# Dense matmul steps written between making and using the attention splits, two branches merged through DRAM, and the bonus placed one head pair later

## The chip, the cores and the metric

The kernel runs on one core of a Trainium2 chip. The metric is device time in microseconds (us); the median of several runs counts, and one further execution was profiled. Engine names in the profile: PE is TensorE, PEld its weight load, DVE is Vector, ACT is Scalar, POOL is GpSimd, SP the engine whose queue issues all DMAs here.

## What is computed

One layer of a hybrid decoder trunk on 1024 tokens of width 1024: a token mixer, a cross-attention into 256 memory tokens, a gated FFN and a final norm. The change touches the mixer. One projection of the normalised stream feeds three branches (gated convolution, stick-breaking attention, RWKV-7) and three gates:

```python
proj = xn @ w_comb
y_conv = c_b * causal_dwconv(c_c * c_x, conv_w)
y_sb = stick_breaking_attention(to_heads(q), to_heads(k), to_heads(v))
y_rwkv, v_first = rwkv7_time_mix(proj[..., OFF_RWKV:], ...)
gates = sigmoid(proj[..., OFF_GATE:OFF_RWKV].reshape(b, s, 3, D) + gate_b)
branches = einsum("bsnc,ncd->bsnd", ys, branch_proj)
merged = einsum("bsnd,bsnd->bsd", gates, branches)
h = h + merged @ w_mix_out
```

In the attention of a head, row t weights column s < t by sig(z_ts) times the product of 1 - sig(z_tj) for s < j < t. The RWKV branch adds a bonus: sum over a head of r * k * r_k, times v.

## The kernel before

All large products are made in three parts: each fp32 operand is split into a rounded high part (a cast on ACT) and a low part (a subtraction on DVE or POOL), and hi*hi, hi*lo and lo*hi add up in PSUM. `split_tile` (L234, L235) loads and splits a weight tile in two halves, with raised priority; `dense_fm` (L255, L256, L259) writes the matmuls of one tile of 128 columns by 1024 tokens, six of 128x512 for each of `nk` blocks of 128 rows; `proj` does both for a tile of `w_comb` (`nk` = 8). PSUM holds two tiles `pd` of 1024 columns, for dense products, and four `pq` of 512.

The order is a planner's. The framework's planner takes each engine's instructions from a list in the order of the source (moved up by `high_priority`), and issues the first one whose operands and buffers are ready by its own model of times; on the chip each engine then works its list strictly in order, and waits for what is late. The Python order of the calls is therefore the priority of the work.

The mixer runs in these stages:

- RWKV preparation (about 50 to 240 us): for each of four head pairs p, small products (`small`, L366), three projections (`shifted`: k, r, v), Vector and ACT work between them, and at the end of the pair the bonus: `rkh` and `rkl` (L450, L451) are the split of r * k * r_k, two small products with them and a multiply by v (L455) give `bon`, written to DRAM.
- RWKV recurrence (about 240 to 600 us), with 24 filler tiles (`FILL_R`) behind it in the source, 12 gate tiles and 12 of the memory's keys and values, which the planner pulls into its gaps.
- Stick-breaking attention, four head pairs (about 620 to 1207 us). `sb_proj(p)` projects v, k and q of a pair and splits them. `sb_att(p)` goes over 2 heads and 4 row blocks m of 256 rows: `scores` (L814, L815 on PE, sigmoids on ACT, masks on POOL, a scan L825 and a multiply L827 on DVE) makes two tiles Z, and `weighted` (of the block before, by the list `late`) transposes Z (L837), splits it into `ah` (L841, ACT) and `al` (L842, DVE) and multiplies by v (L847, L848). Behind each of the pairs 0 to 2 the source has `sb_proj` of the next pair and `fill(5)`: the other 12 gate tiles and 4 convolution tiles of three projections each. `gate_tile` writes its sigmoid to `gate_d` in DRAM, `conv_tile` its result to `y_d[0]`.
- Before pair 3 the residual tiles `h` (x, 8 of 512 KB) are loaded into the room of `xn`, which is done with. Merge: in the order `MERGE` = conv, RWKV, attention, `branch_y` loads a branch's result from `y_d` and splits it (L746, L747), `branch` makes a product (`nk` = 4) for each of 8 column tiles and loads its gate tile. The first branch's gated tiles stay in SBUF (`acc`, multiply L902), the second's are multiplied (L934) and added on POOL (L935), the third's (`merged`, L943, L944) complete the sum, which is split again (L947, L948) and multiplied by `w_mix_out` in `accumulate`, two tiles at a time, into `h` (L921).

Cross-attention and FFN follow and are left as they are.

## Time and profile before

| | |
|---|---|
| median of 3 runs | 2392.54 us (2390.92 to 2396.98) |
| profiled execution, device time | 2392.83 us |
| its span, first to last instruction | 2390.7 us |
| PE busy (matmuls) | 2232.4 us, 93% |
| DVE busy | 1464.3 us, 61% |
| ACT busy | 894.3 us, 37% |
| POOL busy | 541.3 us, 23% |
| mean granted clock of PE | 0.975 of full speed |
| DMA | 222 MB, 28.6% of the 16 engines' span |

Matmuls overlap in the pipeline, so a row's duration (0.39 us for 128x512) is longer than the distance between two starts; idle time of PE is what no matmul covers. The granted clock is a mean between full (1.0, 2.4 GHz) and half (0.5, 1.2 GHz).

### The profile page before, as it was taken

The page shows a single profiled execution, that of the slowest core. Times are in us where ns is not written, and L with a number is a line of the kernel's source. Part 1 is how long each engine was busy: PE and PEld are TensorE (multiplying, and loading weights), DVE is VectorE, ACT ScalarE, POOL GpSimd, SP SyncE. Part 2 cuts the span into 40 slices and gives each one's busy share as a digit, 9 for nine tenths or more (in the row PEclk, how much of TensorE's full clock was granted, in tenths as well). Part 3 has the DMA queues.
Part 4 walks back from the last instruction along what each step waited for, and adds up shares of the span by engine and source line. Part 5 has one row for each costly group of instructions (what it writes and reads, how often), then busy time and mean ns, then how long its engine had stood idle before and what let it go on. Part 6 is the DMA issues. An engine that isn't in the chain of part 4 may idle for free.

```text
span 2390.7 us, 29984 instructions
## 1 busy us (share of the span) xinstructions
PE 2232.4 (93%) x11635; PEld 1838.1 (77%) x11635; DVE 1464.3 (61%) x2017; ACT 894.3 (37%) x1493; POOL 541.3 (23%) x465
## 2 busy tenths in 40 slices
PE   6998899999989898999799999998699999999998
PEld 5776788878868687788677888886588888877887
DVE  7566555673281816311856675547988888867535
ACT  6643233434362625311622134224444444442212
POOL 1123221222121222122212000001644444413000
PEclk9999999999999999999999999999799999999999
DMA  4323534522302121112465112101322222155211
GB/s 152 128 93 128 192 96 122 155 72 93 93 18 80 36 71 54 55 60 71 154 216 163 56 32 68 32 26 71 89 88 80 87 82 80 62 171 186 96 42 71
DMA packets 225792, 222.15 MB, mean 93 GB/s; under 512 B 34804, under 2 KB 187634, under 8 KB 224626
## 3 DMA queue, kind: packets, MB, share of 16 engines
q1 hardware_dynamic: 225649, 220.24, 28.6%
q8 instruction: 91, 1.49, 0.3%
q14 instruction: 52, 0.42, 0.1%
HBM read 162.00 MB, written 58.20 MB: 92 GB/s over the span
## 4 chain that ended last, share of the span: by engine, by line
PE 69%; DVE 13%; issue 9%; ACT 3%; DMA 3%; POOL 2%; SPq 0%; POOLq 0%; DVEq 0%; ACTq 0%
PE pd L255 8%; PE pd L256 7%; PE pd L259 7%; PE pd L915 5%; PE pd L916 5%; PE pd L919 5%; PE pd L1174 3%; PE pd L1176 3%; PE pd L1175 3%; PE pq L1176 2%; PE pq L1174 2%; PE pq L1175 2%; DVE B L825 2%; DVE wl L235 1%; PE pq L848 1%
## 5 line engine op out<-in xcount | busy, mean ns | idle before, releaser
L255 PE MATMUL pd<-xn_hi,wh 128*128 128x512 f32 x960 | 382.1, 398 | 7.4 <-ACT ft L481 7.4
L256 PE MATMUL pd<-xn_lo,wh 128*128 128x512 f32 x960 | 380.1, 396 | 0.0
L234 ACT CAST wh<-wr 128x512 fp32r<-128x512 f32 x270 | 158.8, 620 | 517.3 <-issue 179.2
L259 PE MATMUL pd<-xn_hi,wl 128*128 128x512 f32 x960 | 306.0, 396 | 0.1
L235 DVE TENSOR_TENSOR wl<-wr,wh 128x512 fp32r<-128x512 f32 x166 | 127.2, 790 | 189.7 <-ACT wh L234 189.5
L235 POOL TENSOR_TENSOR wl<-wr,wh 128x512 fp32r<-128x512 f32 x104 | 139.1, 1354 | 386.3 <-ACT wh L234 383.1
L921 DVE TENSOR_TENSOR h<-pd,h 128x1024 f32<-128x1024 f32 x120 | 146.5, 1220 | 128.8 <-PE pd L919 128.6
L255 PEld LDWEIGHTS pd<-xn_hi,wh 128*128 128x128 f32 x960 | 182.8, 190 | 45.1 <-ACT ft L481 7.8
L256 PEld LDWEIGHTS pd<-xn_lo,wh 128*128 128x128 f32 x960 | 182.8, 190 | 36.3
L259 PEld LDWEIGHTS pd<-xn_hi,wl 128*128 128x128 f32 x960 | 180.7, 190 | 37.5 <-POOL wl L235 0.8
L915 PE MATMUL pd<-wh,ah 128*128 128x512 f32 x352 | 139.6, 397 | 9.5 <-DVE h L921 5.7
L916 PE MATMUL pd<-wl,ah 128*128 128x512 f32 x352 | 139.3, 396 | 1.8 <-DVE wl L1254 1.8
L1168 DVE TENSOR_TENSOR wp<-ws,wp 128x512 fp32r<-128x512 f32 x88 | 120.9, 1374 | 2.4 <-ACT wp L1167 1.8
L1174 PE MATMUL pd<-b,wp 128*128 128x512 f32 x264 | 106.8, 405 | 3.9 <-ACT wp L1167 2.4
L919 PE MATMUL pd<-wh,al 128*128 128x512 f32 x352 | 110.0, 394 | 0.0
L1174 PE MATMUL pq<-t,wp 128*128 128x512 f32 x264 | 103.1, 391 | 2.9 <-ACT wp L1167 2.9
L1111 POOL TENSOR_TENSOR t<-h,t 128x512 fp32r<-128x512 f32 x12 | 17.7, 1482 | 385.1 <-ACT t L1110 385.1
L1227 POOL TENSOR_TENSOR h<-h,h 128x1024 f32<-128x1024 f32 x22 | 52.8, 2400 | 227.7 <-DVE h L1192 193.1
L1176 PE MATMUL pd<-b,wp 128*128 128x512 f32 x264 | 104.0, 394 | 0.2 <-DVE wp L1168 0.2
L1175 PE MATMUL pd<-b,wp 128*128 128x512 f32 x264 | 104.0, 394 | 0.0
L1175 PE MATMUL pq<-t,wp 128*128 128x512 f32 x264 | 102.9, 390 | 0.0
L1167 ACT CAST wp<-ws 128x512 fp32r<-128x512 f32 x88 | 54.7, 622 | 128.5 <-POOL ws L1160 65.8
(366 smaller groups left out, 5154.1 us busy)
## 6 DMA issues: line engine op xcount, KB each, us to landing
wr<-in_w_comb_dram SPq DMA_DIRECT2D x124, 256.0 KB
raw<-in_ffn_up_dram SPq DMA_DIRECT2D x88, 256.0 KB
gate_d<-ft SPq DMA_DIRECT2D x24, 512.0 KB
hid_d<-h SPq DMA_DIRECT2D x22, 512.0 KB
wr<-in_ffn_down_dram SPq DMA_DIRECT2D x42, 256.0 KB
t<-hid_d SPq DMA_DIRECT2D x21, 512.0 KB
wr<-in_ca_wkv_dram SPq DMA_DIRECT2D x32, 256.0 KB
gt<-gate_d SPq DMA_DIRECT2D x16, 512.0 KB
```

Source lines behind the costliest of these rows:

```text
L234: s_.copy(hi[:, sl], raw)
L235: (v_ if lo_e == "dve" else g_).tensor_tensor(lo[:, sl], raw, f32(hi[:, sl]), ALU.subtract)
L255: pe.matmul(o, wh(k), xh(k, h), start=k == 0, stop=False)
L256: pe.matmul(o, wh(k), xl(k, h), start=False, stop=False)
L259: pe.matmul(o, wl(k), xh(k, h), start=False, stop=k == nk - 1)
L915: pe.matmul(ps[:, cs], ah[:, tk], wh[:, cs], start=k == 0, stop=False)
L916: pe.matmul(ps[:, cs], ah[:, tk], wl[:, cs], start=False, stop=False)
L919: pe.matmul(ps[:, cs], al[:, tk], wh[:, cs], start=False, stop=k == n - 1)
L921: v_.tensor_tensor(h[i], ps, h[i], ALU.add)
L1174: pe.matmul(ps, wh[:, k, :], xh[:, k, :], start=k == 0, stop=False)
L1175: pe.matmul(ps, wh[:, k, :], xl[:, k, :], start=False, stop=False)
L1176: pe.matmul(ps, wl[:, k, :], xh[:, k, :], start=False, stop=k == 3)
```

## The change

- **Bonus.** The bonus of RWKV head pair p becomes a function that is called after the k projection of pair p + 1; the last one is called after the loop.
- **Dense steps.** `dense_steps` is `dense_fm` as a generator that yields after each block of six matmuls. `conv_tile`, `sb_proj` and the gate tiles become jobs: a column of `w_comb` and a function that uses the product. `Stream` holds a list of jobs, loads the next job's weights when it begins one, and `beside(work)` runs a generator and, at each of its yields, as many dense steps as its rate says; what is left at the end follows. `sb_att` is a generator that yields after each `scores` (16 times a pair) and inside `weighted` (20 times). `weighted` now makes the transposes and split of turn jj + 1 before the products of turn jj and yields in between.
- **Order.** Behind the recurrence stand only the 24 tiles of `FILL`. Beside pair p stand the jobs of `FILL_S[p]`: p is a projection of the next pair, g a gate tile, c a convolution tile of three projections; 12, 12 and 9 projections. All weight splits of these have their low part on POOL; before, those of `sb_proj` were on DVE.
- **Merge.** Beside pair 3 run the products of the first two branches (conv and RWKV): their inputs `y0` and `y2` lie in the room of `xn`, with six buffers `mt`; each gated product is written to `acc_d` in DRAM (16 of 512 KB). `h` is now loaded after pair 3, in the room of `y2`. `merged` loads both tiles from `acc_d` (16 reads), adds them on POOL and goes on as before; `mg` has 6 buffers instead of 4.

```diff
-FILL = "gm" * 12 + "g" * 12 + "cccc"
-FILL_R = 24
-FILL_S = 5
+FILL = "gm" * 12
+FILL_S = ("pcpgpcgg", "pcpgpcgg", "pgpgpgggg")
        ...
+        acc_d = dram.tile([2, KD, P, T], F32, name="acc_d")
        ...
+        def dense_steps(ps, wh, wl, xh, xl, nk):
+
+            for k in range(nk):
+                for h in range(2):
+                    o = ps[:, h * 512:(h + 1) * 512]
+                    pe.matmul(o, wh(k), xh(k, h), start=k == 0, stop=False)
+                    pe.matmul(o, wh(k), xl(k, h), start=False, stop=False)
+                for h in range(2):
+                    o = ps[:, h * 512:(h + 1) * 512]
+                    pe.matmul(o, wl(k), xh(k, h), start=False, stop=k == nk - 1)
+                yield k
        ...
                 k = shifted(4 + p, 4 + p, "k")
+                if bonus:
+                    bonus.pop()()
        ...
-                bon = kp.tile([P, T], F32, name="gt", bufs=2)
-                small(lambda t, ps: v_.tensor_tensor(bon[:, t], ps, vv[:, t], ALU.mult),
-                      (bmr, rkh), (bmr, rkl))
-                dma(bon_d[:, p, :], bon)
+                def add_bonus(p=p, rkh=rkh, rkl=rkl, vv=vv):
+                    bon = kp.tile([P, T], F32, name="gt", bufs=2)
+                    small(lambda t, ps: v_.tensor_tensor(bon[:, t], ps, vv[:, t], ALU.mult),
+                          (bmr, rkh), (bmr, rkl))
+                    dma(bon_d[:, p, :], bon)
+                bonus.append(add_bonus)
+            bonus.pop()()
        ...
+        def conv_jobs(j):
        ...
+            return [(W + j * P, first), (2 * W + j * P, second), (j * P, third)]
+        def gate_job(n, j):
+            def use(ps):
+                t = ftp.tile([P, T], F32, name="ft")
+                s_.activation(t, ps, AF.Sigmoid, bias=col("gate_b", n * KD + j))
+                dma(gate_d[n, j], t)
+
+            return OFF_GATE + n * D + j * P, use
        ...
+        def proj_run(job):
+            c0, use = job
+            def load():
+                return split_tile(wf, w_comb[:, :, c0:c0 + P], [P, KD, P], lo_e="pool")
+            def run(w):
+                ps = PD()
+                yield from dense_steps(ps, lambda k: w[0][:, k, :], lambda k: w[1][:, k, :],
+                                       lambda k, h: xn_hi[:, k, h * 512:(h + 1) * 512],
+                                       lambda k, h: xn_lo[:, k, h * 512:(h + 1) * 512], KD)
+                use(ps)
+            return load, run, KD
+        class Stream:
+            def __init__(self, jobs, yields):
+                self.jobs = list(jobs)
+                self.rate = sum(n for _, _, n in jobs) / yields
+                self.due = 0.0
+                self.now = None
+                self.next = self.jobs[0][0]()
+            def step(self):
+                while True:
+                    if self.now is None:
+                        if not self.jobs:
+                            return False
+                        w = self.next
+                        run = self.jobs.pop(0)[1]
+                        if self.jobs:
+                            self.next = self.jobs[0][0]()
+                        self.now = run(w)
+                    if next(self.now, "end") != "end":
+                        return True
+                    self.now = None
+            def beside(self, work):
+                for _ in work:
+                    self.due += self.rate
+                    while self.due >= 1:
+                        self.due -= 1
+                        self.step()
+                while self.step():
+                    pass
        ...
-            def branch(n, j, y, wpool, rpool, tag):
        ...
+            def branch_steps(n, j, w, y, rpool, tag):
        ...
-                ps = proj(wp, OFF_SB + 1024 + p * P)
        ...
+                return [(OFF_SB + 1024 + p * P, use_v), (OFF_SB + 512 + p * P, use_k),
+                        (OFF_SB + p * P, use_q)]
        ...
             def weighted(p, h, m, Zs, vt, yo):
-                po = PQ()
-                for jj in range(m + 1):
+                def turn(jj):
                     ps = PQ()
                     for j2 in range(2):
                         j = 2 * jj + j2
        ...
                     al = sp.tile([P, 512], F32R, name="al", bufs=3)
                     s_.copy(ah, ps)
                     v_.tensor_tensor(al, ps, f32(ah), ALU.subtract)
+                    return ah, al
+                cur = turn(0)
+                yield
+                po = PQ()
+                for jj in range(m + 1):
+                    nxt = turn(jj + 1) if jj < m else None
+                    ah, al = cur
                     for j2 in range(2):
                         j = 2 * jj + j2
                         lv = vt[:, j, h].rearrange("p x d -> p (x d)")
        ...
                         pe.matmul(po[:, 0:256], lv, ah[:, sl], start=j == 0, stop=False)
                         pe.matmul(po[:, 0:256], lv, al[:, sl], start=False,
                                   stop=j == 2 * m + 1)
+                    if nxt is not None:
+                        yield
+                    cur = nxt
        ...
-            def flush(keep=0):
-                while len(late) > keep:
-                    weighted(*late.pop(0))
-            def sb_att(p, vt, ks, qh, ql):
+            def sb_att(p, d):
                 yo = sp.tile([P, T], F32, name="yo", bufs=1)
                 for h in range(2):
                     for m in range(4):
        ...
                         for i in (2 * m, 2 * m + 1):
                             Z = sp.tile([P, T], F32, name="Z", bufs=4)
                             B = sp.tile([P, T], F32, name="B", bufs=2)
-                            scores(i, P * (i + 1), Z, B, qh[h], ql[h], ks[h])
+                            scores(i, P * (i + 1), Z, B, d["qh"][h], d["ql"][h], d["ks"][h])
                             Zs.append(Z)
-                        late.append((p, h, m, Zs, vt, yo))
-                        flush(1)
-            cur = sb_proj(0)
+                            yield
+                        if late:
+                            yield from weighted(*late.pop())
+                        late.append((p, h, m, Zs, d["vt"], yo))
+                if p == 3:
+                    yield from weighted(*late.pop())
+            YIELDS = 2 * 8 + 2 * 10
+            cur = {}
+            Stream([proj_run(job) for job in sb_jobs(0, cur)], 1).beside(())
             for p in range(3):
-                sb_att(p, *cur)
-                if p == 2:
-                    flush()
-                    s0.close()
-                cur = sb_proj(p + 1)
-                fill(FILL_S)
-            fill(len(fillers))
+                after = {}
+                ahead = sb_jobs(p + 1, after)
+                jobs = []
+                for o in FILL_S[p]:
+                    if o == "p":
+                        jobs.append(ahead.pop(0))
+                    elif o == "g":
+                        jobs.append(gate_job(*gates.pop(0)))
+                    else:
+                        jobs += [convs.pop(0) for _ in range(3)]
+                Stream([proj_run(job) for job in jobs], YIELDS).beside(sb_att(p, cur))
+                cur = after
             xst.close()
-            hp = pool(root, "h", side=RIGHT)
-            h = [hp.tile([P, D], F32, name=f"h{i}") for i in range(NT)]
-            for i in range(NT):
-                dma(h[i], A["x"][0, i * P:(i + 1) * P, :])
-            sb_att(3, *cur)
-            flush()
-            mrg = ExitStack()
-            accp = pool(mrg, "mac", side=RIGHT)
-            acc = [accp.tile([P, T], F32, name=f"acc{j}") for j in range(KD)]
-            yp = pool(mrg, "my", side=RIGHT)
-            y = branch_y(yp, ftp, "ft", MERGE[0])
-            for j in range(KD):
-                ps, gt = branch(MERGE[0], j, y, wf, ftp, "ft")
-                v_.tensor_tensor(acc[j], ps, gt, ALU.mult)
+            s0.close()
+            m0 = ExitStack()
+            y2 = y_tiles(pool(m0, "my2", side=RIGHT))
+            y0 = y_tiles(pool(m0, "my0", side=RIGHT))
+            mt = pool(m0, "mt", 6, side=RIGHT)
+            branch_y(*y0, mt, "mt", MERGE[0])
+            branch_y(*y2, mt, "mt", MERGE[1])
+            def merge_run(x, j):
+                n, y = MERGE[x], (y0, y2)[x]
+                def run(w):
+                    for jj in (j, j + 1):
+                        ps, gt = yield from branch_steps(n, jj, w, y, mt, "mt")
+                        v_.tensor_tensor(gt, ps, gt, ALU.mult)
+                        dma(acc_d[x, jj], gt)
+                return lambda: branch_w(n, j, wf), run, 8
+            Stream([merge_run(x, j) for x in range(2) for j in range(0, KD, 2)],
+                   YIELDS + 5).beside(sb_att(3, cur))
+            m0.close()
+        hp = pool(root, "h", side=RIGHT)
+        h = [hp.tile([P, D], F32, name=f"h{i}") for i in range(NT)]
+        for i in range(NT):
+            dma(h[i], A["x"][0, i * P:(i + 1) * P, :])
        ...
-        mp = pool(mix, "mg", 4)
+        mp = pool(mix, "mg", 6)
+        mrg = ExitStack()
+        yp = pool(mrg, "my", side=RIGHT)
         wp = pool(mrg, "wm", 3, side=RIGHT)
-        with ExitStack() as st:
-            y = branch_y(pool(st, "my2"), mp, "gt", MERGE[1])
-            for j in range(KD):
-                ps, gt = branch(MERGE[1], j, y, wf, mp, "gt")
-                v_.tensor_tensor(gt, ps, gt, ALU.mult)
-                g_.tensor_tensor(acc[j], acc[j], gt, ALU.add)
         with ExitStack() as st:
             ap = pool(st, "ma", 4)
             n = MERGE[2]
-            y = branch_y(yp, mp, "gt", n)
+            y = y_tiles(yp)
+            branch_y(*y, mp, "gt", n)
+            bw = {}
             def merged(j):
-                ps, gt = branch(n, j, y, wp, mp, "gt")
+                if j % 2 == 0:
+                    bw[0] = branch_w(n, j, wp)
+                a0, a1 = (mp.tile([P, T], F32, name="gt") for _ in range(2))
+                dma(a0, acc_d[0, j])
+                dma(a1, acc_d[1, j])
+                g_.tensor_tensor(a0, a0, a1, ALU.add)
+                ps, gt = run_all(branch_steps(n, j, bw[0], y, mp, "gt"))
                 v_.tensor_tensor(gt, ps, gt, ALU.mult)
-                v_.tensor_tensor(gt, acc[j], gt, ALU.add)
+                v_.tensor_tensor(gt, a0, gt, ALU.add)
                 mh = ap.tile([P, T], F32R, name="mh")
                 ml = ap.tile([P, T], F32R, name="ml")
                 s_.copy(mh, gt)
```

## Rows read from the trace of the kernel before

**Rows 1.** Page, parts 1, 2 and 5: busy us (share) xcount; tenths; groups

```profile
PE 2232.4 (93%) x11635; PEld 1838.1 (77%) x11635; DVE 1464.3 (61%) x2017; ACT 894.3 (37%) x1493; POOL 541.3 (23%) x465
...
PE   6998899999989898999799999998699999999998
...
L235 DVE TENSOR_TENSOR wl<-wr,wh 128x512 fp32r<-128x512 f32 x166 | 127.2, 790 | 189.7 <-ACT wh L234 189.5
```

**Rows 2.** Windows, pairs 0-2: stretch, us; per engine busy (count); PEclk, DMA share, GB/s

```profile
653.00:710.00 57.00, 47.61 (x258) 38.10 (x258) 49.28 (x57) 36.56 (x79) 19.11 (x42) 0.97 0.07 19
...
sum 176.00, PE 147.99 PEld 118.51 DVE 148.59 ACT 108.58 POOL 49.04; mean PE 49.33 PEld 39.50 DVE 49.53 ACT 36.19 POOL 16.35
```

**Rows 3.** Windows between and behind the attention of pairs 0-2, columns as before

```profile
710.00:779.00 69.00, 69.00 (x311) 57.62 (x310) 13.07 (x15) 18.70 (x28) 10.50 (x10) 0.98 0.22 73
...
sum 311.00, PE 311.00 PEld 258.89 DVE 57.51 ACT 75.66 POOL 58.80; mean PE 103.67 PEld 86.30 DVE 19.17 ACT 25.22 POOL 19.60
```

**Rows 4.** PE waits, pairs 0, 1, 3: engine line <- releaser: us, times, longest

```profile
PE pq L848 <- DVE al L842: 8.1, 5, 3.1
...
PE pq L848 <- DVE al L842: 8.9, 7, 2.1
...
PE pq L848 <- DVE al L842: 9.2, 6, 2.6
```

**Rows 5.** Timeline of PE, pair 0: start us, us, what [idle before <-releaser]

```profile
678.47 0.39 PE L848 MATMUL pq<-al,vt 128*128 128x256 f32 x1 [2.23 <-DVE al L842]
...
680.16 0.63 PE L256 MATMUL pd<-xn_lo,wh 128*128 128x512 f32 x1
```

**Rows 6.** Lines, PE, 1000 to 1090 us: shapes xcount | busy us, mean ns

```profile
L255 PE MATMUL pd<-xn_hi,wh 128*128 128x512 f32 x133 | 51.7, 389 | 0.0
```

**Rows 7.** Timeline of POOL, then DVE: beside attention and alone

```profile
704.82 4.85 POOL L235 TENSOR_TENSOR wl<-wr,wh 128x512 fp32r<-128x512 f32 x2 [0.66 <-ACT wh L234]
...
1010.62 2.54 POOL L235 TENSOR_TENSOR wl<-wr,wh 128x512 fp32r<-128x512 f32 x2 [8.34 <-ACT wh L234]
...
675.54 2.29 DVE L825 TENSOR_TENSOR_SCAN B<-B 128x1024 f32<-128x1024 f32 x1 [0.18 <-POOL B L822]
...
705.23 3.38 DVE L825 TENSOR_TENSOR_SCAN B<-B 128x1024 f32<-128x1024 f32 x1
```

**Rows 8.** Windows of pair 3 and the merge behind it

```profile
1140.00:1215.00 75.00, 60.81 (x323) 49.73 (x322) 63.04 (x77) 40.92 (x88) 17.05 (x39) 0.93 0.43 148
1215.00:1310.00 95.00, 91.17 (x396) 73.68 (x395) 56.54 (x54) 23.70 (x32) 19.87 (x8) 1.00 0.63 206
```

**Rows 9.** Tiles acc and ft: xcount: ns min/median/max, first to last start

```profile
L902 DVE TENSOR_TENSOR acc<-pd,ft x8: 1212/1222/1225, 1181.5 to 1236.7; 128x1024 f32<-128x1024 f32 x8
...
L746 ACT CAST yh<-ft x4: 1046/1048/1051, 1139.1 to 1172.5; 128x1024 fp32r<-128x1024 f32 x4
L747 DVE TENSOR_TENSOR yl<-ft,yh x4: 1215/1226/1322, 1140.2 to 1173.8; 128x1024 fp32r<-128x1024 f32 x4
```

**Rows 10.** Chain that ended last, in order of time: start us, us, what

```profile
1226.17 7.09 DMA gt<-y_d
...
1266.42 3.96 DMA gt<-y_d
```

**Rows 11.** Timeline of ACT, then DVE, at the end of pair 3

```profile
1206.80 0.36 ACT L852 COPY tp<-pq 64x256 f32<-64x256 f32 x1 [1.84 <-PE pq L848]
...
1207.19 0.43 DVE L853 TENSOR_TENSOR yo<-pq,tp 64x256 f32<-64x256 f32 x1 [0.24 <-ACT tp L852]
```

**Rows 12.** Window in which the residual tiles are loaded

```profile
1143.00:1160.00 17.00, 12.11 (x65) 8.97 (x63) 15.32 (x20) 11.01 (x24) 6.72 (x14) 1.00 1.01 378
```

**Rows 13.** PE waits in the RWKV preparation, 75 to 245 us

```profile
PE pq L366 <- ACT rkh L450: 10.4, 4, 3.0
PE pq L366 <- DVE rkl L451: 4.9, 3, 1.7
```

**Rows 14.** Window of the second head pair of the RWKV preparation

```profile
110.00:152.00 42.00, 37.94 (x169) 30.82 (x168) 29.39 (x33) 20.63 (x26) 9.29 (x3) 0.96 0.36 122
```

161 lines of the change are left out of this document (84 added, 77 removed).

## The prediction

> **What bounds the kernel now.** I read the page first. TensorE is busy for 93% of the span [rows 1], so time can come only from stretches in which TensorE stands still or runs at half its clock. The 40 slices of 59.8 us point to where: of those that the diff touches, PE falls to 8 tenths in the fourth (179 to 239 us, RWKV preparation) and in the twelfth, fourteenth and sixteenth (attention of head pairs 0 to 2), and to 7 in the twentieth (1136 to 1195 us, pair 3) [rows 1].
>
> The windows of the first three head pairs come next. Three stretches, the first from 653 to 710 us and the two others like it, 176 us in all, hold 148.0 us of PE and as much Vector work, 49.5 us each [rows 2]. So 28.0 us of PE is idle and Vector, at 84%, is the tight engine. Between and behind them lie three stretches of projections, 311 us, in which PE has no gap and Vector is busy for 57.5 us [rows 3]: the planner has already pulled some dense work into the attention, but most is left in blocks where Vector has nothing to do. The waits name the cause: in each stretch 8 to 9 us (8.1 in pair 0, 8.9 in pair 1, and as much in pair 2) go to the second matmul of `weighted` (L848), which waits for the low half `al` that Vector makes at L842, at most 3.1 us at a time in pair 0 and 2.1 in the others [rows 4]. The timeline shows one: L848 stands 2.23 us for `al`, and a dense matmul behind it then takes 0.63 us [rows 5], where the mean of its kind in a dense stretch is 0.39 [rows 6]: the half clock, 1.2 GHz instead of 2.4. The granted mean is 0.97 in these stretches [rows 2]; a mean of 0.97 between full and half is a loss of 3% of the time.
>
> **Part 1: dense steps in between (pairs 0 to 2).** Nothing is removed: 33 projections, their splits and the attention stay. What moves is the place of each. A dense step is six 128x512 matmuls; 133 of each of its three lines (one row stands for three) fill the 90 us from 1000 to 1090 [rows 6], so one takes 0.226 us, a step 1.35 us, a projection of 8 steps 10.8 us. Pairs 0 and 1 get 12 projections (96 steps, 130 us) over 36 points at which the attention yields, 2.67 steps or 3.6 us each; pair 2 gets 72 steps, 2.0 or 2.7 us each. The new `weighted` makes the split of turn jj+1 and yields before it uses turn jj, so 2.7 to 3.6 us of other PE work stands where the longest waits were 3.1 and 2.1 us. Vector's 49.5 us then lie in a stretch of 125 to 155 us, not 59.
>
> What can be won is the idle 28.0 us, 3% of 176 us = 5.3 us of slow clock [rows 2], and 2% of the 143 us of the first two dense stretches, both at 0.98 [rows 3], = 2.9 us: 36 us. What stays: the weight splits' subtractions of the 12 query, key and value projections move from Vector to POOL (`lo_e="pool"`), and all POOL subtractions now run beside attention. A pair of them takes 2.54 us in a dense stretch and 4.85 us beside attention, and a 1024-long scan that overlaps them takes 3.38 us instead of 2.29 [rows 7]. I leave 6 us for such late splits and for the tails of the streams: gain 30 us, bounds 18 and 36 (no loss at the lower end, because the dense steps lie ahead of the waiting matmul in the queue, not behind it).
>
> The Trainium skill has a rule that speaks against this part: in "SBUF — State Buffer", section "Who interferes with whom", a Vector instruction with two SBUF inputs and a GpSimd instruction that reads SBUF exclude each other, the later one blocked until the first is done. The scan of [rows 7] agrees with that.
>
> A rival follows from the row alone: if about a third of a pair's 24 half subtractions held a Vector instruction for the 1.1 us that the scan shows [rows 7], and each delay came through to PE, 9 us a pair would be lost, 27 in all. It is called "port" below.
>
> **Part 2: branches beside pair 3.** Before, the stretch 1140 to 1215 has 75 - 60.8 = 14.2 us of idle PE and a clock of 0.93, 5.2 us more: 19.4 us [rows 8]. After, 16 branch products of 4 steps (87 us) are spread over it at 1.56 steps, 2.1 us, per yield. This cover is thinner than the longest wait there, 2.6 us [rows 4]. Vector also carries more here: the attention's 49.5 us, 16 multiplies of 1.22 (L902's kind) and eight `yl` of 1.23 [rows 9], and 16 half weights of 0.79 [rows 1]: some 91 us in some 117. And both branches' inputs are split at the start, ahead of the first scores in source order: four casts of 1.05 and four subtractions of 1.23 [rows 9] before the first branch is whole, with only `weighted` of pair 2 as cover. I leave 4 us for that start and 6 us for Vector: gain 9 us, bounds 0 and 17. The multiplies were there before; the 16 writes of 512 KB to `acc_d` are new. SP issues them in order with the gate loads, each after its multiply; six `mt` buffers hold the loads ahead, so I cost them at nothing. Without that cover each late gate load would cost a landing, 4 to 7 us [rows 10].
>
> **Part 3: the boundary behind pair 3.** Before, the last `yo` was made at 1207.6 us [rows 11] and the other branch's 43 us of products hid its way to DRAM and back; PE idled only 95 - 91.2 = 3.8 us from 1215 to 1310 [rows 8]. After, both hidden branches are used up when attention ends. The last `y_d` write, its read (a 512 KB load cost the chain 4.0 to 7.1 us [rows 10]; the write is not shown alone, and I take 4 for it), the copy and addition ahead of it (0.36 and 0.43 [rows 11]) and one cast and subtraction (2.3) make a chain of 11 us. The other three quarters of the SB input can feed 3 steps of each of two merged tiles, 8 us, if they are there in time. But the residual tiles `h` now take the room of `y2` and so are loaded only here, eight of 512 KB: at the 378 GB/s of the stretch where they run now [rows 12], 4.2 MB are 11 us, and source order puts them ahead of the y loads. Behind those come a gate and two `acc_d` tiles for each of the first two merged tiles, 3.1 MB, 8 us. Bounds: 11 - 8 = 3 us idle, about what it is now (a gain of at most the 3.8 us), up to 11 + 11 + 8 = 30 us, 26 more than now. `mg` overlays the attention's `yo` and `Z` tiles, so the y loads can hardly run early; I take 17 us, 13 more than now. Later `acc_d` reads (8.4 MB over some 130 us) and the POOL additions, eight as before, lie a pair of tiles ahead of PE; I cost them at nothing (a late one costs its landing, 4 to 7 us).
>
> **Part 4: the bonus.** PE waits 10.4 us for `rkh` and 4.9 for `rkl` at the bonus matmuls, in four head pairs, up to 3.0 us at a time [rows 13]; the next pair's first matmuls are queued behind. A pair later, both are long made. Three of four pairs profit (the last still comes right behind its split): 3/4 of 15.3 us is 11.5 us, and a clock of 0.96 over the 42 us of the second pair and the 43 of the third (their rows are alike [rows 14]) is 3.4 us. Vector is at 29.4 of 42 us there [rows 14], so part may turn up as another wait in the chain of a pair: 11 us, bounds 4 and 15.
>
> **Sum.** Against the profiled execution, 2392.8 us (span 2390.7), which lies 0.3 us above the median: 2392.8 - 30 - 9 + 13 - 11 = 2356 us.
>
> **Rivals.** *Boundary dear*: the forecast, but the boundary costs 27 more than now: 2370. For it: source order and the 512 KB loads; against: loads are issued when their tile is free, so some may pass. *Boundary hidden*: boundary 0, parts 1, 2 and 4 at 33, 15 and 13: 2332. For it: three quarters of the input exist early. *Port*: part 1 gives 9 instead of 30 us: 2377. *Planner*: the change doesn't do what it says, since the framework's planner orders PE by readiness in its own model and not by source; the first branch product's multiply ran at 1181.5 us [rows 9], inside pair 3, though its code stands behind it. If it pulls the dense steps forward, Vector stays tight: part 1 gives 10, part 2 nothing: 2385. Against: the model was early with L848, so it sees everything as ready, and ready work keeps source order. *Slower*: in pair 3, SP holds each gate load behind an `acc_d` write that waits for its multiply; 16 loads late by 4.0 us [rows 10] are 64 us on PE, so 2356 + 64 = 2420. It ends slower than before once a load comes more than 37/16 = 2.3 us late. Against: six buffers instead of two.
>
> **How the numbers follow.** Forecast 0.50 (its own range 2344 to 2368), boundary dear 0.17, boundary hidden 0.10, port 0.08, planner 0.09, slower 0.06. The range 2328 to 2388 takes in all but the slower rival and the ends of the bounds. A difference under 0.3%, 7 us, can hardly be told from no change: faster by more than that holds for all but the slower rival and half of the planner's, 0.88; same 0.06, slower 0.06.
>
> **What would show it.** Right: L848 waits of under 3 us per pair, granted clock 0.99 or more from 650 to 1100 us, Vector under 50% there; one PE gap of 10 to 25 us, with a clock dip, right after pair 3, ended by a load of `y_d` or `acc_d` or by a cast; L366 waits under 6 us in all. Wrong: PE gaps inside pairs 0 to 2 as large as now; PE waiting in pair 3 for gate tiles; no gap at the boundary; a new wait on L408 or L255 in the RWKV preparation.

## The result, and the profile after

The changed kernel takes 2367.2 us (median, 2366.9 to 2373.4) where the kernel before took 2393.1 in the same session: a ratio of 0.9896, 95% interval 0.9876 to 0.9917, so 25.8 us or 1.1% less. The forecast was 2356, in the range of 2328 to 2388; the time lies inside the forecast's own range (2344 to 2368), at its upper end, and 3 us from the rival *boundary dear* (2370). The profiled execution has a span of 2365.2 us, against 2390.7 before.

The page of the changed kernel, parts 1 and 2 (busy us, share of the span and instructions; then busy tenths in 40 slices of 59.1 us), to be read beside [rows 1]:

```profile
PE 2209.7 (93%) x11635; PEld 1828.4 (77%) x11635; DVE 1463.5 (62%) x1993; ACT 896.0 (38%) x1493; POOL 571.0 (24%) x489
...
PE   6999899999999999998958999996899999989998
```

The slices of attention (the eleventh to the eighteenth) now all show 9, where before the twelfth, fourteenth and sixteenth showed 8. But the twenty-first, 1183 to 1242 us, shows 5, lower than any slice of before. That is the whole result in one line: a gain in pairs 0 to 2, and a hole behind pair 3.

Stage by stage, from the starts of named matmuls in the two traces (us from the start of the span):

| mark | before | after | stage before | stage after | difference |
|---|---|---|---|---|---|
| last bonus matmul | 235.2 | 219.9 | 235.2 | 219.9 | -15.3 |
| first scores of attention | 653.1 | 635.4 | 417.9 | 415.5 | -2.4 |
| last projection of the mixer | 1140.5 | 1078.0 | 487.4 | 442.6 | -44.8 |
| first product with `w_mix_out` | 1302.6 | 1270.1 | 162.1 | 192.1 | +30.0 |
| last product with `w_mix_out` | 1416.8 | 1386.9 | 114.2 | 116.8 | +2.6 |
| first product with the memory's keys (cross-attention) | 1440.5 | 1414.9 | 23.7 | 28.0 | +4.3 |
| end | 2390.7 | 2365.2 | 950.2 | 950.3 | +0.1 |

Not all of the 44.8 us is won. The stage behind the last projection has 727 matmul records and had 690; 37 matmuls at 0.23 us, some 8 us of PE work, have only crossed the mark, and are part of the 30.0.

Lines have moved: L255, L256 and L259 of before are L275, L276 and L279 in the dense steps (L256, L257 and L260 where `dense_fm` is still used), L366 is L387, L408 is L433, L842 is L944, L848 is L958, L746 and L747 are L834 and L835, L921 is L1054, L943 is L1080.

**Pairs 0 to 2.** The window of the changed kernel from the first scores to the last projection (length; busy us and count of PE, PEld, DVE, ACT, POOL; granted clock; DMA share; GB/s), and what PE waited for in it (us in sum, times, longest):

```profile
635.00:1078.00 443.00, 438.93 (x2179) 367.61 (x2178) 203.96 (x219) 181.00 (x335) 126.68 (x182) 1.00 0.19 60
```

```profile
PE pq L958 <- DVE al L944: 4.0, 4, 1.4
```

Against [rows 2] and [rows 3]: 4.1 us of idle PE where there were 28.0; a clock of 1.00 where 0.97 and 0.98 were granted; Vector's work spread evenly, 46% of the stretch and not 84% of a part of it. The waits for `al`, 8 to 9 us in each pair [rows 4], are 4.0 us for all three.

**The bonus.** Windows of the RWKV preparation, from the first small product to the last bonus matmul, of the kernel before and then of the changed one, and the waits left in it after:

```profile
72.60:235.20 162.60, 147.28 (x656) 119.34 (x655) 104.09 (x114) 80.87 (x101) 40.25 (x15) 0.97 0.32 110
```

```profile
72.20:219.90 147.70, 142.38 (x657) 117.13 (x656) 103.90 (x114) 80.21 (x101) 39.40 (x15) 1.00 0.35 120
```

```profile
PE pq L387 <- ACT rkh L475: 2.4, 1, 2.4
PE pq L387 <- DVE rkl L476: 1.7, 1, 1.7
PE pq L433 <- ACT kkr L427: 1.2, 1, 1.2
```

Idle PE falls from 15.3 to 5.3 us, and the clock goes from 0.97 to 1.00, 3% of 162.6 = 4.9 us: together the 14.9 us by which the window is shorter. Of [rows 13] the one wait of the last pair is left, 4.1 us, and there is a new one of 1.2 us, for `kkr`, whose transposes (L433) now stand right behind the bonus. (A new wait at this line, L408 before, was one of the prediction's signs of being wrong; it is a small one.)

**Behind pair 3.** Windows of the changed kernel: pair 3, the hole, the first two merged tiles:

```profile
1078.00:1217.00 139.00, 125.58 (x630) 104.15 (x629) 88.33 (x103) 53.34 (x105) 15.54 (x39) 0.98 0.52 179
1217.00:1245.00 28.00, 0.00 (x0) 0.00 (x0) 5.31 (x7) 4.36 (x7) 0.00 (x0) 0.56 0.86 298
1245.00:1290.00 45.00, 40.64 (x165) 32.31 (x166) 33.40 (x26) 10.42 (x13) 14.39 (x6) 0.93 0.78 283
```

In the hole no engine computes to speak of; the DMA engines are busy for 0.86 of it. The timeline of PE (start, us, what, idle time before and its releaser) shows its ends, and that the first matmuls behind it run at the half clock, 0.63 us and not 0.39:

```profile
1216.38 0.61 PE L279 MATMUL pd<-yh,wl 128*128 128x512 f32 x2
1245.44 1.22 PE L275 MATMUL pd<-yh,wh 128*128 128x512 f32 x2 [28.44 <-ACT yh L834]
...
1247.29 0.63 PE L275 MATMUL pd<-yh,wh 128*128 128x512 f32 x1
```

The timeline of SP's queue says what the transfers are (start and length of the issue, what, how many):

```profile
1215.14 0.32 SPq L969 DMA_DIRECT2D y_d<-yo  x1
1217.03 0.33 SPq L1034 DMA_DIRECT2D h<-in_x_dram  x1
1218.29 0.32 SPq L1024 DMA_DIRECT2D acc_d<-mt  x1
1218.66 1.47 SPq L1034 DMA_DIRECT2D h<-in_x_dram  x2
1220.18 2.17 SPq L233 DMA_DIRECT2D wr<-in_branch_proj_dram  x3
1222.39 0.49 SPq L1034 DMA_DIRECT2D h<-in_x_dram  x1
1227.62 0.37 SPq L233 DMA_DIRECT2D wr<-in_branch_proj_dram  x1
1228.25 1.02 SPq L233 DMA_DIRECT2D wr<-in_w_mix_out_dram  x2
1229.33 0.42 SPq L1034 DMA_DIRECT2D h<-in_x_dram  x1
1231.88 1.53 SPq L233 DMA_DIRECT2D wr<-in_w_mix_out_dram  x2
1235.13 0.38 SPq L233 DMA_DIRECT2D wr<-in_branch_proj_dram  x1
1235.56 1.41 SPq L1034 DMA_DIRECT2D h<-in_x_dram  x3
1237.01 2.08 SPq L833 DMA_DIRECT2D gt<-y_d  x4
```

The attention's result is asked for 22 us after it was written, behind 18 other transfers. Ahead of its first tile, its own write counted, stand eight `h` (4.2 MB), two writes (1.0) and nine half weights (2.4); with that tile itself 8.1 MB, which at the 298 GB/s of the window take 27 us.

That rate is a mean with pauses. In the rows above SP issues nothing from 1222.9 to 1227.6, from 1229.8 to 1231.9 and from 1233.4 to 1235.1 us: each time it stands before the load of a half weight until one of the three raw buffers `wr` of `split_tile` is free again (9.7 us of waits at L233 from 1217 to 1238 us), and issues nothing that stands behind that load. From 1236 to 1250 us, without such a pause, the rate was 364 GB/s at a DMA share of 0.97. With the DMA engines busy for 0.86 of the 28 us, the pauses can account for some 4 us of the hole by this count; no run has more raw buffers, so their part is not measured. The cast of the first tile is the releaser of PE:

```profile
1244.34 1.04 ACT L834 CAST yh<-gt 128x1024 fp32r<-128x1024 f32 x1 [9.96 <-DMA gt<-y_d]
```

### The profile page after: what moved, and what is told of

Read it like the earlier page. It is cut to its first block, busy times and chain, and to the rows that moved or that the text cites. A ratio compares the mean times of both kernels' runs of the same rounds, so it can differ in the third digit from the quotient of the medians.

```text
span 2365.2 us, 30012 instructions
## 1 busy us (share of the span) xinstructions
PE 2209.7 (93%) x11635; PEld 1828.4 (77%) x11635; DVE 1463.5 (62%) x1993; ACT 896.0 (38%) x1493; POOL 571.0 (24%) x489
## 4 chain that ended last, share of the span: by engine, by line
PE 74%; DVE 14%; issue 4%; ACT 3%; DMA 3%; POOL 1%; SPq 0%; DVEq 0%; POOLq 0%; ACTq 0%
PE pd L275 6%; PE pd L276 6%; PE pd L279 6%; PE pd L1048 5%; PE pd L1049 5%; PE pd L1052 5%; PE pd L1311 4%; PE pd L1312 3%; PE pd L1313 3%; PE pd L256 3%; PE pd L260 3%; PE pd L257 3%; PE pq L1311 3%; PE pq L1312 3%; PE pq L1313 3%
## 5 line engine op out<-in xcount | busy, mean ns | idle before, releaser
L236 POOL TENSOR_TENSOR wl<-wr,wh 128x512 fp32r<-128x512 f32 x128 | 176.8, 1399 | 280.6 <-ACT wh L235 274.3
L275 PE MATMUL pd<-xn_hi,wh 128*128 128x512 f32 x576 | 227.7, 395 | 0.0
L276 PE MATMUL pd<-xn_lo,wh 128*128 128x512 f32 x576 | 225.0, 391 | 0.0
L1054 DVE TENSOR_TENSOR h<-pd,h 128x1024 f32<-128x1024 f32 x120 | 146.4, 1220 | 123.7 <-PE pd L1052 123.5
L279 PE MATMUL pd<-xn_hi,wl 128*128 128x512 f32 x576 | 178.3, 390 | 0.0
L256 PE MATMUL pd<-xn_hi,wh 128*128 128x512 f32 x384 | 154.2, 402 | 6.1 <-ACT ft L519 6.1
L236 DVE TENSOR_TENSOR wl<-wr,wh 128x512 fp32r<-128x512 f32 x142 | 108.6, 787 | 71.2 <-ACT wh L235 71.0
L257 PE MATMUL pd<-xn_lo,wh 128*128 128x512 f32 x384 | 151.7, 395 | 0.0
L927 DVE TENSOR_TENSOR_SCAN B<-B 128x128 f32<-128x128 f32 (+3 forms) x64 | 86.9, 1358 | 88.6 <-POOL B L924 88.5
L279 PEld LDWEIGHTS pd<-xn_hi,wl 128*128 128x128 f32 x576 | 108.0, 188 | 23.6 <-POOL wl L236 0.2
L276 PEld LDWEIGHTS pd<-xn_lo,wh 128*128 128x128 f32 x576 | 108.3, 188 | 19.7
L275 PEld LDWEIGHTS pd<-xn_hi,wh 128*128 128x128 f32 x576 | 108.2, 188 | 19.5
L260 PE MATMUL pd<-xn_hi,wl 128*128 128x512 f32 x384 | 121.9, 397 | 0.1
L944 DVE TENSOR_TENSOR al<-pq,ah 128x512 fp32r<-128x512 f32 x80 | 54.6, 688 | 91.5 <-ACT ah L943 91.1
L1311 PE MATMUL pd<-b,wp 128*128 128x512 f32 x264 | 107.1, 406 | 2.4 <-ACT wp L1304 2.4
L275 PE MATMUL pd<-yh,wh 128*128 128x512 f32 x192 | 77.1, 404 | 31.7 <-ACT yh L834 28.4
```

What stands on the lines that cost most here:

```text
L236: (v_ if lo_e == "dve" else g_).tensor_tensor(lo[:, sl], raw, f32(hi[:, sl]), ALU.subtract)
L256: pe.matmul(o, wh(k), xh(k, h), start=k == 0, stop=False)
L257: pe.matmul(o, wh(k), xl(k, h), start=False, stop=False)
L260: pe.matmul(o, wl(k), xh(k, h), start=False, stop=k == nk - 1)
L275: pe.matmul(o, wh(k), xh(k, h), start=k == 0, stop=False)
L276: pe.matmul(o, wh(k), xl(k, h), start=False, stop=False)
```

## Theories

*Queue and bytes* (mine, after the traces): what is won in pairs 0 to 2 and by the bonus is larger than forecast; the merge gives most of the forecast back and more, because 25 MB (`h`, weights, y, gate tiles, two `acc_d` tiles for each column tile) must come in through one stretch at some 300 GB/s, while the PE work that used to cover them was moved ahead, beside pair 3. Two forms of it must be told apart: the *order* alone (the few tiles that PE needs first stand behind others), which another order would mend, and the *bytes* in all, which it would not.

Rivals: the *round trip* of the last quarter through DRAM makes the hole; *port*, GpSimd's subtractions hold Vector back; *planner*, the gain in pairs 0 to 2 does not come from the split made ahead, since the planner fills waits by itself.

All ratios are to the kernel before, run on the same chip. In some profiled executions the recurrence, the same code, ended 5 us later than in others (the last section); so the stretch from the first scores to the last product with `w_mix_out`, "the mixer's stretch", is given too: 763.7 us before, 751.5 after.

## Which parts win, which lose

**The bonus alone**, in the kernel before:

```diff
                 k = shifted(4 + p, 4 + p, "k")
+                if bonus:
+                    bonus.pop()()
...
-                bon = kp.tile([P, T], F32, name="gt", bufs=2)
+                def add_bonus(p=p, rkh=rkh, rkl=rkl, vv=vv):
+                    bon = kp.tile([P, T], F32, name="gt", bufs=2)
...
+                bonus.append(add_bonus)
+            bonus.pop()()
```

> The kernel before with the bonus a head pair later and nothing else. Theory (the bonus part gives what the two traces show up to the first scores, 15.4 us in the preparation and 2.9 us more in the recurrence): 2375 us, waits at the bonus matmuls 4 us in all instead of 15.3. Rival (part of that gain is the planner's other order further on, not the bonus): 2382 us, my forecast's 11 us.

2377.7 us, ratio 0.9933 (0.9918 to 0.9948): 15.3 us less, nearer the theory than the rival. The last bonus matmul starts at 220.2, as in the changed kernel. The whole of the gain ahead of the attention is the bonus; it was mis-sized low.

**The changed kernel with the merge of before** (the bonus and the streams of pairs 0 to 2 stay; `h` is loaded before pair 3, the first two branches run behind it, their sums stay in SBUF):

```diff
-            m0 = ExitStack()
-            y2 = y_tiles(pool(m0, "my2", side=RIGHT))
...
-            Stream([merge_run(x, j) for x in range(2) for j in range(0, KD, 2)],
-                   YIELDS + 5).beside(sb_att(3, cur))
+            for i in range(NT):
+                dma(h[i], A["x"][0, i * P:(i + 1) * P, :])
+            for _ in sb_att(3, cur):
+                pass
...
+            for j in range(KD):
+                ps, gt = branch(MERGE[0], j, y, wf, ftp, "ft")
+                v_.tensor_tensor(acc[j], ps, gt, ALU.mult)
```

> The changed kernel with the merge of before: residual tiles loaded before pair 3, no dense steps written into pair 3, branch sums kept in SBUF. Theory (the merge part loses what the boundary gap costs; bonus 18 us and pairs 0 to 2 about 40 us stand by themselves): 2393 - 18 - 40 = 2335 to 2340 us, no PE gap over 3 us behind pair 3. Rival (the branches beside pair 3 pay for the gap, or the pairs' gain is only my 30 us): 2350 to 2367 us.

2341.2 us, ratio 0.9779 (0.9764 to 0.9793): faster than both kernels, and 1 us above the range of the theory. From this run and the one ahead of it the three parts can be told apart by medians (the changed kernel was timed in another session, in which the kernel before gave the same 2393.1 us): bonus -15.3 (2393.1 to 2377.7), streams -36.6 (2377.7 to 2341.2), new merge +26.0 (2341.2 to 2367.2); in sum -25.9.

The windows from the last projection to the first product with `w_mix_out`, in the changed kernel and with the old merge:

```profile
1078.00:1270.10 192.10, 150.21 (x727) 123.84 (x727) 111.76 (x124) 64.36 (x119) 22.75 (x42) 0.90 0.61 213
```

```profile
1078.10:1248.90 170.80, 153.96 (x726) 124.99 (x725) 115.88 (x129) 68.11 (x125) 35.61 (x47) 0.95 0.55 179
```

The same matmuls (727 and 726 records) with 41.9 us of idle PE and with 16.8: the new merge adds 25.1 us of standing still and takes 3.8 us off the busy time, 21.3 in sum (the rest of the 26.0 is mostly the later start of cross-attention, +4.3 in the table). Two further windows of the run with the old merge say why: pair 3 without cover, then the two branches in the open behind it.

```profile
1070.00:1149.00 79.00, 62.85 (x339) 50.16 (x338) 62.77 (x79) 44.50 (x92) 15.95 (x40) 0.91 0.39 130
1149.00:1249.00 100.00, 98.31 (x428) 80.81 (x427) 55.90 (x54) 24.89 (x35) 19.87 (x8) 0.98 0.63 205
```

Pair 3 without cover loses 16.2 us idle and 9% of 79 = 7.1 us of clock, 23 us; with the branches beside it the changed kernel still loses 13.4 us and 2% of 139 = 2.8, 16 us. So, with the clock's share reckoned as lost time, putting 87 us of products beside pair 3 won some 7 us. And behind pair 3 the old order loses 1.7 us in 100, under loads of 205 GB/s: the products that were moved away had been the cover of these loads.

**One branch beside pair 3** (the same kernel, but the first branch's products written as dense steps beside pair 3, the sums still in SBUF):

```diff
-            for _ in sb_att(3, cur):
-                pass
...
-            for j in range(KD):
-                ps, gt = branch(MERGE[0], j, y, wf, ftp, "ft")
-                v_.tensor_tensor(acc[j], ps, gt, ALU.mult)
+            Stream([merge_run(j) for j in range(0, KD, 2)], YIELDS + 5).beside(sb_att(3, cur))
```

> e2 with the products of the first branch written beside pair 3 as dense steps (32 steps, 0.78 per yield), its sum kept in SBUF, the second branch's products behind attention as before, the residual tiles loaded before pair 3. No DRAM for the sums and 43 us of cover at the boundary. Theory (the dense steps between make and use are worth having in pair 3 as well when nothing is paid at the boundary): the 15 us of gaps in pair 3 of e2 fall to 9 or 10: 2335 us. Rival (the planner already pulls these products in): 2341 us, no change.

2363.2 us (0.9868, 0.9842 to 0.9894), 22 us more than without it: both expectations fell. Pair 3 and the hole behind it (1078 to 1199 us) keep 28.1 us of idle PE at a clock of 0.90:

```profile
1078.00:1199.00 121.00, 92.90 (x465) 75.10 (x463) 75.92 (x92) 50.43 (x102) 16.01 (x40) 0.90 0.40 135
...
1199.38 1.22 PE L274 MATMUL pd<-yh,wh 128*128 128x512 f32 x2 [11.06 <-ACT yh L833]
```

The trace divides them. About 12.6 lie from 1083 to 1116 us, before the first branch's products run, since the split of their input is finished only then; the old merge has 10.3 idle in the same part of pair 3 (1078 to 1109 us), so nothing is won there. In the 72 us behind it, with the dense steps (43 us over 41 yields, 1.05 us each), 4.8 us are idle at a clock of 0.95. The last 11.1 are a new gap: the branch's products are then missing in front of the second branch's loads, with neither `h` nor `acc_d` in the way. What a moved product covered at its old place counts as much as what it covers at the new one.

## What the hole behind pair 3 is made of

**Another result to load** (round trip or queue): the third merge reads the convolution's result in place of the attention's.

```diff
-            branch_y(*y, mp, "gt", n)
+            branch_y(*y, mp, "gt", 0)
```

> The changed kernel, but the last merge reads the convolution's result, which lies in DRAM since about 1000 us, in place of the attention's (so the merged sum holds the convolution branch where the attention belongs; bytes, queue order and products are the same). If the gap behind pair 3 is the round trip of the attention's last quarter through DRAM, the loads no longer depend on it: gap under 22 us instead of 28.4, total 2361 or less. If it is what stands ahead of these loads in SP's order (the residual tiles and the weight loads, 17 MB at about 300 GB/s), the gap stays at 26 to 30 us and the total at 2364 to 2370 us. I expect the latter.

2369.5 us (0.9918, 0.9901 to 0.9934), as expected, and the gap is no smaller, though the last write of this data was issued at 927.5 us, 300 us earlier:

```profile
1247.19 1.22 PE L275 MATMUL pd<-yh,wh 128*128 128x512 f32 x2 [29.37 <-ACT yh L834]
```

The round trip does not make the hole; what stands ahead of these loads on the queue does, by its order or by its bytes.

**The residual tiles loaded later**, behind the first two merged tiles in source order:

```diff
-        for i in range(NT):
-            dma(h[i], A["x"][0, i * P:(i + 1) * P, :])
...
             acts = [merged(0), merged(1)]
+            for i in range(NT):
+                dma(h[i], A["x"][0, i * P:(i + 1) * P, :])
```

> The changed kernel with the eight loads of the residual tiles written behind the first two merged tiles, so that SP issues the y loads before them. Theory (queue order: the y loads stand 20 us behind h and weight loads on SP): the PE gap falls from 28.4 to 10 to 13 us, 2350 to 2354 us. Rival (round trip: the last y_d write, its read and the split make the gap): gap over 22 us, 2362 us or more.

2371.7 us (0.9912, 0.9896 to 0.9929): no gain, where order alone had promised 13 to 17 us. The time is the rival's (2362 or more), the gap (over 22 us) is not. Its PE timeline, and the place of `h` on its SP queue:

```profile
1230.22 0.80 PE L275 MATMUL pd<-yh,wh 128*128 128x512 f32 x1 [10.81 <-ACT wh L235]
...
1246.39 0.47 PE L275 MATMUL pd<-yh,wh 128*128 128x512 f32 x1 [3.49 <-DVE gt L1078]
...
1272.68 0.76 PE L1046 MATMUL pd<-wh,mh 128*128 128x512 f32 x1 [13.49 <-DVE gt L1078]
...
1247.72 3.12 SPq L1088 DMA_DIRECT2D h<-in_x_dram  x6
```

The first gap fell by 17.6 us, as it should; but 17.8 us of gaps stand behind it (3.5, 13.5 and 0.8), where the changed kernel has 3.9, since the third merged tile's `acc_d` and gate loads now come after `h`, and after a half weight for which SP stood from 1250.8 to 1260.2 us. The wait wandered by one stage.

**The residual tiles from another queue** (GpSimd issues them):

```diff
-            dma(h[i], A["x"][0, i * P:(i + 1) * P, :])
+            nc.gpsimd.dma_start(h[i], A["x"][0, i * P:(i + 1) * P, :])
```

> The changed kernel, but the eight loads of the residual tiles h are issued from GpSimd's queue instead of SP's, so that the attention's result and the weights no longer stand behind them in order, while the bytes moved in the same stretch stay the same. If only the order on SP's queue costs, the first gap falls from 28.4 to 12 us or less and no other takes its place: total 2355 or less. If the bytes cost, because all loads share about 300 GB/s, the 4.2 MB still take their 14 us from the loads that TensorE waits for: gaps of 20 us or more in sum from 1217 to 1275 us, total 2358 to 2368 us. I lean to the second.

2369.1 us (0.991, 0.9895 to 0.9925), 1 us above the range expected for the bytes. The attention's result is now asked for 3.5 us after its write, but the window of the merge's start is no shorter in bytes:

```profile
1217.00:1275.00 58.00, 32.85 (x117) 24.71 (x116) 30.96 (x28) 13.74 (x18) 14.12 (x12) 0.77 0.89 312
...
1235.26 0.80 PE L275 MATMUL pd<-yh,wh 128*128 128x512 f32 x1 [17.42 <-ACT wh L235]
```

PE is idle for 25.2 us of this window, with gaps of 17.4, 3.4 and 3.2 us and some short ones, and the changed kernel's gaps are 32.3; yet the mixer's stretch is 750.4 us, 1 us less. The clock took the difference: behind the first gap both traces have 592 matmuls up to the last product with `w_mix_out`, busy for 136.4 us at a granted clock of 0.98 in the changed kernel and for 141.4 us at 0.95 here, where waits and short pieces of work alternate. A queue of its own is no bandwidth of its own. The Trainium skill says so in "DMA: Bandwidth & Descriptors", section "Issuing engines are not separate DMA queues": the transfers run on the same 16 DMA engines whoever starts them. The trace agrees: 312 GB/s here, 296 in the same window of the changed kernel.

**No residual loads at all** (`h` is set to zero on GpSimd, so the residual is missing from the output):

```diff
-            dma(h[i], A["x"][0, i * P:(i + 1) * P, :])
+            g_.memset(h[i], 0.0)
```

> The changed kernel without the eight loads of the residual tiles (4.2 MB; zeros written by POOL instead, so the residual is left out). New theory (bytes: 17.2 MB pass between the end of pair 3 and the first products with w_mix_out, in this kernel and in e3 alike, at about 300 GB/s, and PE has 22 us of work for them): 4.2 MB less are 11 to 14 us: 2353 to 2356 us. Rival (waits in SP's queue, one load behind another's buffer, whatever the bytes): under 5 us gain, 2362 us or more.

2358.8 us (0.9851, 0.9824 to 0.9877), between the two expectations and nearer the bytes', and 741.4 us for the mixer's stretch, 10 less than the changed kernel. The gaps up to 1280 us are 17.6 us in sum where the changed kernel has 32.3; the difference is 14.7, and 4.2 MB at 296 GB/s are 14 us.

```profile
1231.98 0.79 PE L275 MATMUL pd<-yh,wh 128*128 128x512 f32 x1 [9.97 <-ACT wh L235]
...
1248.62 0.47 PE L275 MATMUL pd<-yh,wh 128*128 128x512 f32 x1 [3.60 <-DVE gt L1080]
...
1268.25 0.77 PE L1048 MATMUL pd<-wh,mh 128*128 128x512 f32 x1 [4.03 <-DVE gt L1080]
```

**No `acc_d` reads** (the 8.4 MB and GpSimd's additions are left out, so two branches are missing from the sum):

```diff
-                a0, a1 = (mp.tile([P, T], F32, name="gt") for _ in range(2))
-                dma(a0, acc_d[0, j])
-                dma(a1, acc_d[1, j])
-                g_.tensor_tensor(a0, a0, a1, ALU.add)
...
-                v_.tensor_tensor(gt, a0, gt, ALU.add)
```

> The changed kernel without the 16 reads of acc_d and the POOL additions (the two hidden branches are left out of the sum; the writes stay). Bytes: of 8.4 MB about 4.2 fall in the 58 us behind pair 3, so again 11 to 14 us: 2353 to 2356 us. Rival (order: the y loads still stand behind the h loads on SP): gap still 25 us or more, 2362 us or more.

2366.7 us (0.9882, 0.9858 to 0.9907), mixer's stretch 746.7, 5 less. Twice the bytes of `h`, half its price:

```profile
1251.92 1.22 PE L275 MATMUL pd<-yh,wh 128*128 128x512 f32 x2 [29.56 <-ACT yh L834]
1282.38 0.50 PE L1048 MATMUL pd<-wh,mh 128*128 128x512 f32 x1 [0.49 <-DVE h L1054]
```

The reads stand behind the attention's result, so the first gap stays; what goes are the small gaps behind it. In these runs bytes cost what stands ahead of PE's next need, less what PE has to do meanwhile. Neither plain form holds: order alone fell with the two runs that move `h`, and bytes alone, as I had put it for this run (2353 to 2356), fell here.

**More cover**: the branches' products are spread over 56 yields instead of 41, so that some are left when attention ends:

```diff
-                   YIELDS + 5).beside(sb_att(3, cur))
+                   YIELDS + 20).beside(sb_att(3, cur))
```

> The changed kernel with the stream beside pair 3 spread over 56 instead of 41 yields, so that 18 of 64 dense steps, 24 us, are left when attention ends. Both theories: the y chain runs beside these steps. Queue order: the weights of the first merged tile still come behind the h loads, so a gap of about 8 us stays, and thinner cover costs 4 us in attention: 2351 us. Round trip: the gap goes altogether, 2343 us.

2358.2 us (0.9845, 0.9829 to 0.9862), mixer's stretch 737.6, 14 less; both expectations (2351 and 2343) were too low. The first gap is ended by a weight cast, and gaps of 2.9 and 2.0 us follow:

```profile
1235.59 0.79 PE L275 MATMUL pd<-yh,wh 128*128 128x512 f32 x1 [11.88 <-ACT wh L235]
```

**More cover, and the merged tiles' weights from the pool that is free earlier**:

```diff
-                   YIELDS + 5).beside(sb_att(3, cur))
+                   YIELDS + 20).beside(sb_att(3, cur))
...
-                    bw[0] = branch_w(n, j, wp)
+                    bw[0] = branch_w(n, j, wf)
```

> e4 with the weights of the merged tiles in the pool wf, so that their loads need not wait for the mt tiles. Queue order of the weights as the cause of e4's last gap of 11.9 us: gap under 4 us, 2349 us. Bytes: the 24 us of cover carry some 7 MB of the 17, the rest still needs time beside the 22 us of merged tiles, so part of the gap turns up again at later loads: 2352 to 2356 us.

2354.6 us (0.9836, 0.9814 to 0.9858), as expected for the bytes; mixer's stretch 737.4, no better than cover alone in the trace. The gap is now ended by the gate multiply (L1080), whose load comes last:

```profile
1253.50 0.77 PE L275 MATMUL pd<-yh,wh 128*128 128x512 f32 x1 [15.32 <-DVE gt L1080]
```

With 319 GB/s moved from 1222 to 1270 us, the wait found another last load.

## What the gain in pairs 0 to 2 is made of

**No split ahead**: streams and yields stay; the transposes and the split of a turn are written right before its products.

```diff
-                cur = turn(0)
+                cur = None
                 yield
...
-                    nxt = turn(jj + 1) if jj < m else None
-                    ah, al = cur
+                    nxt = jj < m or None
+                    ah, al = turn(jj)
```

> The changed kernel with the same streams and the same yields, but the transposes and the split of a turn are written right before the products that use them, not one yield ahead. If the split made ahead is what removed the waits for al (8 to 9 us per head pair before, 1.0 to 1.35 now), they return: 6 us or more in each of the four pairs, with the clock below 0.99 there, total 2385 to 2400 us. Rival: it is enough that the dense work is spread over the attention and Vector has less to do at a time; then the waits for al stay under 3 us per pair and the total at 2365 to 2375 us. I lean to the first.

2380.2 us (0.9957, 0.9941 to 0.9974), 13 more than the changed kernel; by the traces 8 (end at 2373.4), of which 6.9 in pairs 0 to 2 (442.6 to 449.5 us). Time lies between the two expectations, the mechanism is the rival's: the waits for `al` did not come back (0.7 us in all). One turn in the changed kernel, PE's timeline, and one in this:

```profile
706.46 0.60 PE L939 MATMUL pq<-ident,Z 128*128 128x128 f32 x4
706.82 0.36 PE L957 MATMUL pq<-ah,vt 128*128 128x256 f32 x1
707.02 0.28 PE L958 MATMUL pq<-al,vt 128*128 128x256 f32 x1
```

```profile
707.04 0.60 PE L939 MATMUL pq<-ident,Z 128*128 128x128 f32 x4
707.40 0.48 PE L275 MATMUL pd<-xn_hi,wh 128*128 128x512 f32 x1
...
708.41 0.35 PE L957 MATMUL pq<-ah,vt 128*128 128x256 f32 x1
708.60 0.63 PE L279 MATMUL pd<-xn_hi,wl 128*128 128x512 f32 x2
709.10 0.39 PE L958 MATMUL pq<-al,vt 128*128 128x256 f32 x1
```

The planner pulls dense matmuls in between by itself; that a dense step already begun is at hand there is my reading of it. As far as this run tells, some 7 to 13 of the 36.6 us come from the split ahead, and the rest, by subtraction, from the even spread of dense work. The loss of this run hides in the busy time:

```profile
635.00:1086.00 451.00, 448.87 (x2180) 361.67 (x2179) 207.69 (x219) 181.17 (x334) 128.46 (x182) 1.00 0.19 59
```

As many matmuls as in the changed kernel's 443 us, a higher busy share (99.5% against 99.1%), and 8 us longer. Counted by the distances between starts, delays under 0.45 us sum to 22.6 us in 443, against 13.3 in the changed kernel (both sums shift with the distance that is taken as usual for a shape; the difference stays at 9 to 10). A matmul that is a tenth of a us late or less starts inside the modelled tail of the one before, and no row shows a gap: the L958 at 709.10 follows two matmuls that take 0.23 us each from start to start elsewhere, after 0.50.

**The low parts on Vector** instead of GpSimd:

```diff
-                return split_tile(wf, w_comb[:, :, c0:c0 + P], [P, KD, P], lo_e="pool")
+                return split_tile(wf, w_comb[:, :, c0:c0 + P], [P, KD, P])
```

> The changed kernel, but the low parts of the weight splits of pairs 0 to 2's streams (66 half tiles) are made on Vector instead of GpSimd: 66 x 0.79 = 52 us more on Vector over 443 us (from 46% to 58%). My rival port says that GpSimd's subtractions hold Vector's scans and splits back beside the attention; if that came through to TensorE, taking them away gives back the small gaps and slow clock still there, 5 us or more: 2362 or less. Otherwise TensorE covers it either way: 2364 to 2372 us, no difference from the changed kernel beyond 4 us. I expect the latter.

2370.8 us (0.9915, 0.9895 to 0.9935), pairs 0 to 2 in 443.1 us against 442.6: no difference. The move itself is visible in this run's window, whose counterpart of the changed kernel has 205.3 us of Vector and 126.7 of GpSimd:

```profile
635.00:1080.00 445.00, 440.59 (x2187) 368.92 (x2186) 237.38 (x284) 183.33 (x337) 39.21 (x120) 1.00 0.19 60
```

The rival *port* falls. The rule of the Trainium skill that spoke against this part ("SBUF — State Buffer", "Who interferes with whom") is not refuted: the longest scans took 2.47 us in the mean in the stretch of before, but 2.29 in the changed kernel and 2.29 here. In the changed kernel it is GpSimd that takes longer: its 62 subtractions of weights take 1.44 us in the mean, half of the undisturbed pair of [rows 7] is 1.27. TensorE lost nothing by it that this run could give back.

## Why the prediction came out as it did

The direction and the range held; the forecast missed by 11 us. That it did not miss by 22 is luck: the merge was mis-sized by that much, and the other two parts, each mis-sized the other way, gave 11 of it back. The terms against what the runs gave:

| term of the sum | forecast | measured | from |
|---|---|---|---|
| part 1, streams in pairs 0 to 2 | -30 (-18 to -36) | -36.6 | old merge less bonus alone |
| parts 2 and 3, branches beside pair 3 and boundary | +4 | +26.0 | changed kernel less old merge |
| part 4, bonus | -11 (-4 to -15) | -15.3 | bonus alone |

- **Part 1** was right in its mechanism and mis-sized: 6 us set aside for late splits and tails were not lost. Signs as predicted: waits for `al` under 3 us a pair, clock 1.00, Vector at 46%. (A slip without a visible cost: pair 0 has 32 yields, not 36, because its first `scores` have no `weighted` behind them, so a tenth of its stream stands behind it.) The measured 36.6 includes what the new `weighted` does in pair 3 of that run. But the step from "a yield of 3.6 us stands between split and use" to the gain was only part of the cause; the run without the split ahead keeps most of it.
- **Part 2**: 9 us forecast; 7 us by the losses of pair 3 against the old merge in the same kernel (23 there, 16 after), but 3 against the kernel before, whose pair 3 lost 19.4. Where 4 us had been left for its start, 8.7 were lost in seven gaps from 1078 to 1110 us; the later waits for `al` took 4.7 of the 6 us left for Vector. The 3.3 us gap at 1110 is ended by the multiply of a gated product (`mt`, L1023). It looks like the rival *slower*, but Vector has no idle time before that multiply: it stood behind the last splits `yl` of the branches' inputs and two half weights, not behind a gate load. PE waited for no gate tile in pair 3, so six `mt` buffers do what I took them for.
- **Part 3** is the step that failed. I put down 17 us and chose the middle of 3 to 30 us; the gap is 28.4, with 3.9 more in two gaps behind. The pieces were all named: chain 11, `h` 11, `acc_d` and gates 8. What I got wrong is the price of order: I let the bytes ahead overlap with the chain and with three quarters of the input that "exist early". On the queue nothing exists early: all four y loads are issued behind the last `h`. Nine half weights, 2.4 MB, which I had not counted, stand there too, and the mean rate, with SP's pauses before half weights, was 298 GB/s, not the 378 of [rows 12]: 8.1 MB at 298 GB/s are 27 us. The upper bound of 30 held for the first gap, not for all three (32.3); the sign given, one gap of 10 to 25 us, did not hold.
- Costed at nothing, and not nothing: the `acc_d` reads behind the first gap (5 us by the run without them) and the start of cross-attention (+4.3 us, 2.1 of them in one gap before its first transposes; the old merge has 23.6 us there as before, so it belongs to the new merge, but by which path is open).
- **Part 4**: the waits went as predicted and the clock too. The 4 us held back for another wait in a pair's chain were too many; 1.2 us turned up. The upper bound, 15, was the time.
- **Rivals**: *boundary dear* is what happened at the boundary (27 more forecast for it, 26 measured for the merge as a whole), while part 1 and the bonus beat the forecast by 11. *Port* fell with the run on Vector, the round trip with the other result to load, *boundary hidden* with the 28 us hole. *Planner* is refuted in its result (part 1 gave more, not 10) but right in its mechanism: the planner does pull ready matmuls ahead. (By the prediction's own chances, faster by more than 7 us adds up to 0.895, not 0.88.)

What stays open: what more raw buffers `wr` would give behind pair 3, and why with the old merge the stages from cross-attention on take 3.6 us more in the profiled execution (953.9 against 950.3).
